# Rotary embedding on one core: whole 4 MB batches in five slots in place of 2 MB half batches in nine

## Chip, cores, metric

The kernel runs on one core of one Trainium2 chip. The metric is the device time of one execution in microseconds; most runs of one kernel agree within 0.3%.

## The reference, cut to what matters

```python
# x: (8, 2048, 8, 64) float32; cos, sin: (2048, 32) float32
x1, x2 = x[..., :32], x[..., 32:]
out1 = x1 * cos - x2 * sin        # cos, sin broadcast over batch and head
out2 = x1 * sin + x2 * cos
return np.concatenate([out1, out2], axis=-1)
```

33.55 MB come in, 33.55 MB go out, and the tables are 0.52 MB. Two multiplies and one add per element are all the work.

## The kernel before

Sequence positions lie on the partitions, 16 of them in each, so that one batch is 128 rows of 32 KB. A slab is half of that: 16 KB rows, 2 MB. It is loaded into one of nine slots, computed in place, and stored.

```python
SL = 8; n_half = R // SL; SLAB = SL * HD; UNIT = 4 * HD; NBUF = 9     # HD = 512 columns
slabs = [(b, l) for l in range(n_half) for b in range(B)]             # 16 slabs

def load(i):                       # all loads on the sync queue
    ...
    for lo, n in spans(cuts(i)):   # slab 0 in 256, 256, 512 KB and 1 MB, others whole
        nc.sync.dma_start(out=xt[:, lo : lo + n], in_=xv[b, :, l * SLAB + lo : ...])
        if i == 0 and lo == 0:
            nc.sync.dma_start(out=sin_sb, in_=sin_src)

nc.scalar.dma_start(out=cos_sb, in_=cos_src)
for i in range(NBUF):
    load(i)
```

A tile is 2048 columns (UNIT). There are three kinds. In A, GpSimd makes t2 = x swapped times sin (two instructions), VectorE makes t1 = x times cos and adds them. In B the add is done by TensorE (two products with the identity into PSUM) and ScalarE copies it back. In C VectorE makes both products and TensorE adds; GpSimd has nothing to do.

```python
kinds = {}
for i in (5, 10):
    kinds |= {(i, 0): "C", (i, UNIT): "B"}

def rotate(i, lo, n):
    ...
    if kind != "C":
        for u, tab in ((1, sin_sb), (0, nsin)):
            nc.gpsimd.tensor_mul(out=t2u[...], in0=xu[..., 1 - u, :], in1=rep(tab, H))
    keep(nc.vector.tensor_mul(out=t1, in0=xk, in1=rep(cos_ps, 2 * H)))
    if kind == "A":
        keep(nc.vector.tensor_add(out=xt, in0=t1, in1=t2))
    ...

for i in range(last + 1):          # stores on the ACT queue, two slabs late
    ...
    for lo, n in spans(pieces(i)):
        rotate(i, lo, n)
        if i == last:
            store(i, lo, n)
    if LAG <= i < last:
        store(i - LAG, 0, SLAB)
    if i > LAG and i - LAG - 1 + NBUF <= last:
        load(i - LAG - 1 + NBUF)
```

## Time and profile before

| | before |
|---|---|
| time, median | 164.75 us (164.62 to 164.78) |
| span of the profiled execution | 163.0 us |
| VectorE / GpSimd busy | 143.4 / 139.4 us |
| VectorE's last add ends | 155.0 us |
| transfers between 60 and 150 us | 431 GB/s |

### The profile page before, as it was taken

How to read it: one execution, taken by the hardware profiler on the slowest of the kernel's cores; microseconds unless marked ns; L12 is line 12 of the kernel's file. 1: busy time of each engine (PE TensorE's matmuls, PEld its weight loads, DVE VectorE, ACT ScalarE, POOL GpSimd, SP SyncE). 2: the span in 40 equal slices, each digit the busy share in tenths (PEclk: the TensorE clock that was granted, in tenths of full speed). 3: DMA queues.
4: the chain of work that ended last, by engine and by line, in shares of the span. 5: the costliest groups of instructions: out<-in, count | busy, mean ns of one | idle time of the engine just before them, and what ended most of it. 6: DMA issues, size and time to landing. Idle time of an engine off the chain costs nothing. (4 is left out here: it accounts for less than half of the span.)

```text
span 163.0 us, 480 instructions
## 1 busy us (share of the span) xinstructions
PE 33.3 (20%) x64; PEld 13.4 (8%) x64; DVE 143.4 (88%) x71; ACT 12.0 (7%) x20; POOL 139.4 (86%) x74
## 2 busy tenths in 40 slices
PE   0000000000000079993000000899920000000000
PEld 0000000000000024440000000244400000000000
DVE  0587999999999999999899999999999999999900
ACT  3300000000000002232000000022410000000000
POOL 1599999999999999799999999956999999995000
PEclk9999999999999999999555555579997555555555
DMA  4999999999999999999999999999999999999995
GB/s 137 383 432 442 406 398 426 438 438 418 438 434 426 430 434 430 426 434 438 422 428 438 424 422 446 430 414 446 434 422 430 442 422 422 446 426 430 434 402 207
DMA packets 5763, 67.66 MB, mean 415 GB/s; under 512 B 640, under 2 KB 640, under 8 KB 1664
## 3 DMA queue, kind: packets, MB, share of 16 engines
q1 hardware_dynamic: 2880, 33.82, 49.5%
q10 hardware_dynamic: 2880, 33.82, 48.7%
q14 instruction: 3, 0.02, 0.0%
HBM read 34.08 MB, written 33.55 MB: 415 GB/s over the span
## 5 line engine op out<-in xcount | busy, mean ns | idle before, releaser
L138 POOL TENSOR_TENSOR t<-xt,sin_sb 128x1024 f32<-128x1024 f32 (+2 forms) x34 | 70.7, 2081 | 10.8 <-DVE xt L151 6.3
L144 DVE TENSOR_TENSOR t<-xt,cos_ps 128x2048 f32<-128x2048 f32 (+2 forms) x36 | 73.9, 2056 | 1.0
L138 POOL TENSOR_TENSOR t<-xt,nsin 128x1024 f32<-128x1024 f32 (+2 forms) x34 | 70.8, 2082 | 0.0
L151 DVE TENSOR_TENSOR xt<-t,t 128x2048 f32<-128x2048 f32 (+2 forms) x32 | 64.8, 2025 | 5.6 <-POOL t L138 2.1
L172 PE MATMUL o<-t,eye 128*128 128x512 f32 x16 | 11.3, 800 | 85.8 <-DVE t L144 85.8
L176 ACT COPY xt<-o 128x512 f32<-128x512 f32 x8 | 4.7, 586 | 94.5 <-DVE t L144 55.3
L172 PEld LDWEIGHTS o<-t,eye 128*128 128x128 f32 x16 | 3.9, 256 | 90.6 <-issue 90.6
L156 PE MATMUL o<-t,eye 128*128 128x512 f32 x16 | 8.2, 592 | 0.0
L157 PE MATMUL o<-t,eye 128*128 128x512 f32 x16 | 8.2, 592 | 0.0
L173 PE MATMUL o<-t,neye 128*128 128x512 f32 x8 | 6.2, 862 | 0.2 <-DVE t L161 0.2
L158 ACT COPY xt<-o 128x512 f32<-128x512 f32 x8 | 4.7, 586 | 9.0 <-PE o L157 9.0
L108 DVE COPY cos_ps<-cos_sb 128x512 f32<-128x512 f32 x1 | 0.7, 694 | 5.0 <-DMA cos_sb<-in_cos_dram 5.0
L161 DVE TENSOR_TENSOR t<-xt,sin_ps 128x2048 f32<-128x2048 f32 x2 | 4.6, 2281 | 0.0
L173 PE MATMUL o<-t,eye 128*128 128x512 f32 x8 | 4.1, 592 | 0.0
L157 PEld LDWEIGHTS o<-t,eye 128*128 128x128 f32 x16 | 3.0, 190 | 3.8 <-issue 3.8
L156 PEld LDWEIGHTS o<-t,eye 128*128 128x128 f32 x16 | 3.0, 190 | 3.8 <-issue 3.8
L173 PEld LDWEIGHTS o<-t,neye 128*128 128x128 f32 x8 | 2.0, 278 | 4.9 <-issue 3.3
L173 PEld LDWEIGHTS o<-t,eye 128*128 128x128 f32 x8 | 1.5, 190 | 1.9 <-issue 1.9
L106 ACT ACT_TABLE_LOAD x1 | 1.3, 1283 | 1.2 <-PEq L215 1.2
L106 ACT ACTIVATE nsin<-sin_sb 128x512 f32<-128x512 f32 x1 | 0.6, 630 | 3.2 <-DMA sin_sb<-in_sin_dram 3.2
L109 ACT COPY sin_ps<-sin_sb 128x512 f32<-128x512 f32 x1 | 0.6, 579 | 0.0
L96 POOL MEMSET eye<- 128x128 f32 x1 | 0.2, 205 | 0.3 <-POOLq L215 0.3
(6 smaller groups left out, 1.0 us busy)
## 6 DMA issues: line engine op xcount, KB each, us to landing
xt<-in_x_dram SPq DMA_DIRECT2D x15, 2048.0 KB, 27.6
out_dram<-xt ACTq DMA_DIRECT2D x15, 2048.0 KB, 15.3
xt<-in_x_dram SPq DMA_DIRECT2D x1, 1024.0 KB, 7.8
out_dram<-xt ACTq DMA_DIRECT2D x1, 1024.0 KB, 10.3
xt<-in_x_dram SPq DMA_DIRECT2D x2, 256.0 KB, 4.3
xt<-in_x_dram SPq DMA_DIRECT2D x1, 512.0 KB, 5.8
out_dram<-xt ACTq DMA_DIRECT2D x1, 512.0 KB, 8.9
out_dram<-xt ACTq DMA_DIRECT2D x2, 256.0 KB, 7.6
```

The costliest lines, as they stand in the source:

```text
L106: nc.scalar.mul(nsin, sin_sb, -1.0)
L108: nc.vector.tensor_copy(cos_ps, cos_sb)
L138: nc.gpsimd.tensor_mul(out=t2u[:, :, u, :].rearrange("p (r h) d -> p r h d", h=H), in0=xu[:, :, 1 - u, :].rearrange("p (r h) d -> p r h d" ...
L144: nc.vector.tensor_mul(out=t1.rearrange("p (r k d) -> p r k d", r=nr, d=Dh), in0=xk, in1=rep(cos_ps[:, r0 : r0 + nr, :], 2 * H),)
L151: keep(nc.vector.tensor_add(out=xt, in0=t1, in1=t2))
L156: nc.tensor.matmul(o, eye, t1[:, cs], start=True, stop=False)
L157: nc.tensor.matmul(o, eye, t2[:, cs], start=False, stop=True)
L158: keep(nc.scalar.copy(xt[:, cs], o))
L161: nc.vector.tensor_mul(out=t2.rearrange("p (r k d) -> p r k d", r=nr, d=Dh), in0=xk, in1=rep(sin_ps[:, r0 : r0 + nr, :], 2 * H),)
L172: nc.tensor.matmul(o, eye, t1u[:, gs, u, :], start=True, stop=False)
L173: nc.tensor.matmul(o, eye if u else neye, t2u[:, gs, 1 - u, :], start=False, stop=True)
L176: keep(nc.scalar.copy(xu[:, gs, u, :], o.rearrange("p (g d) -> p g d", d=Dh)))
```

## The change

Its intent: fewer and longer transfers, the first MB of x ahead of the tables, stores as soon as a batch is done, and one TensorE tile in each of batches 1 to 5 rather than two in each of two slabs.

```diff
-    SL = 8 ... SLAB = SL * HD
+    ROW = R * HD
     UNIT = 4 * HD
-    NBUF = 9
+    NBUF = 5
-    t1s_pool = ... bufs=3
+    t1s_pool = ... bufs=2
-    def load(i): ...
-    nc.scalar.dma_start(out=cos_sb, in_=cos_src)
+    def load(b):
+        xt = xpool.tile([P, ROW], f32, tag="xt", name=f"xt{b}")
+        for lo, n in spans([UNIT, UNIT, 2 * UNIT] if b == 0 else [ROW]):
+            keep(nc.sync.dma_start(out=xt[:, lo : lo + n], in_=xv[b, :, lo : lo + n]))
+            if b == 0 and lo == 0:
+                keep(nc.sync.dma_start(out=cos_sb, in_=cos_src))
+                keep(nc.sync.dma_start(out=sin_sb, in_=sin_src))
-    for i in (5, 10):
-        kinds |= {(i, 0): "C", (i, UNIT): "B"}
+    for b, kind in ((1, "C"), (2, "B"), (3, "C"), (4, "B"), (5, "B")):
+        kinds[(b, 0)] = kind
     ...
+    def pieces(b):
+        if b == 0:
+            return [2 * HD, 2 * HD, UNIT, UNIT, UNIT]
+        if b == last:
+            return [UNIT, UNIT, UNIT, 2 * HD, 2 * HD]
+        return [UNIT] * 4
-    LAG = 2 ...
+    for b in range(B):
+        done = 0
+        outs = list(spans([2 * UNIT, UNIT, UNIT] if b == last else [ROW]))
+        for lo, n in spans(pieces(b)):
+            rotate(b, lo, n)
+            done = lo + n
+            while outs and sum(outs[0]) <= done:
+                store(b, *outs.pop(0))
+        if b + NBUF <= last:
+            load(b + NBUF)
```

More of the change, by code (lines that the diff above doesn't have):

```diff
@@ L28 @@
     R = S // P
-    SL = 8
-    n_half = R // SL
-    SLAB = SL * HD
+    ROW = R * HD
     UNIT = 4 * HD
-    NBUF = 9
+    NBUF = 5
     C = 512
+    last = B - 1
     xv = x.rearrange("b (q r) h d -> b q (r h d)", q=P)
@@ L45 @@
     o_pool = ctx.enter_context(tc.tile_pool(name="op", bufs=2, space=PSUM))
-    t1s_pool = ctx.enter_context(tc.tile_pool(name="t1s", bufs=3))
+    t1s_pool = ctx.enter_context(tc.tile_pool(name="t1s", bufs=2))
     xpool = ctx.enter_context(tc.tile_pool(name="xpool", bufs=NBUF))
@@ L56 @@
     sin_ps = tab_pool.tile([P, R, Dh], f32, tag="sp")
-    slabs = [(b, l) for l in range(n_half) for b in range(B)]
-    last = len(slabs) - 1
     xts = {}
-    def cuts(i):
-        if i == 0:
-            return [HD, HD, 2 * HD, UNIT]
-        return [SLAB]
-    def pieces(i):
-        if i == 0:
-            return [HD, HD, 2 * HD, UNIT]
-        if i == last:
-            return [UNIT, 2 * HD, HD, HD]
-        return [UNIT, UNIT]
     def spans(sizes):
@@ L78, in spans, with store @@
             lo += n
-    def load(i):
-        b, l = slabs[i]
-        xt = xpool.tile([P, SLAB], f32, tag="xt", name=f"xt{i}")
-        for lo, n in spans(cuts(i)):
-            nc.sync.dma_start(
-                out=xt[:, lo : lo + n],
-                in_=xv[b, :, l * SLAB + lo : l * SLAB + lo + n],
-            )
-            if i == 0 and lo == 0:
-                nc.sync.dma_start(out=sin_sb, in_=sin_src)
-        xts[i] = xt
-    nc.scalar.dma_start(out=cos_sb, in_=cos_src)
-    for i in range(NBUF):
-        load(i)
+    def load(b):
[5 more added lines that the diff above has]
+                keep(nc.sync.dma_start(out=sin_sb, in_=sin_src))
+        xts[b] = xt
+    def store(b, lo, n):
+        keep(nc.scalar.dma_start(out=ov[b, :, lo : lo + n], in_=xts[b][:, lo : lo + n]))
+    for b in range(NBUF):
+        load(b)
     nc.gpsimd.memset(eye, 0.0)
@@ L105 @@
     )
-    nc.scalar.mul(nsin, sin_sb, -1.0)
-    nc.scalar.mul(neye, eye, -1.0)
-    nc.vector.tensor_copy(cos_ps, cos_sb)
-    nc.scalar.copy(sin_ps, sin_sb)
+    keep(nc.scalar.mul(nsin, sin_sb, -1.0))
+    keep(nc.scalar.copy(sin_ps, sin_sb))
+    keep(nc.scalar.mul(neye, eye, -1.0))
+    keep(nc.vector.tensor_copy(cos_ps, cos_sb))
     def rep(a, n):
@@ L114, with rotate @@
     kinds = {}
-    for i in (5, 10):
-        kinds |= {(i, 0): "C", (i, UNIT): "B"}
-    def rotate(i, lo, n):
-        b, l = slabs[i]
-        kind = kinds.get((i, lo), "A")
-        xt = xts[i][:, lo : lo + n]
-        r0 = l * SL + lo // HD
+    for b, kind in ((1, "C"), (2, "B"), (3, "C"), (4, "B"), (5, "B")):
+        kinds[(b, 0)] = kind
+    def rotate(b, lo, n):
+        kind = kinds.get((b, lo), "A")
+        xt = xts[b][:, lo : lo + n]
+        r0 = lo // HD
         nr = n // HD
@@ L137, in rotate @@
             for u, tab in ((1, sin_sb), (0, nsin)):
-                nc.gpsimd.tensor_mul(
-                    out=t2u[:, :, u, :].rearrange("p (r h) d -> p r h d", h=H),
-                    in0=xu[:, :, 1 - u, :].rearrange("p (r h) d -> p r h d", h=H),
-                    in1=rep(tab[:, r0 : r0 + nr, :], H),
+                keep(
+                    nc.gpsimd.tensor_mul(
+                        out=t2u[:, :, u, :].rearrange("p (r h) d -> p r h d", h=H),
+                        in0=xu[:, :, 1 - u, :].rearrange("p (r h) d -> p r h d", h=H),
+                        in1=rep(tab[:, r0 : r0 + nr, :], H),
+                    )
                 )
@@ L175, in rotate @@
                     )
-                    keep(nc.scalar.copy(xu[:, gs, u, :], o.rearrange("p (g d) -> p g d", d=Dh)))
-    LAG = 2
-    def store(i, lo, n):
-        b, l = slabs[i]
-        keep(
-            nc.scalar.dma_start(
-                out=ov[b, :, l * SLAB + lo : l * SLAB + lo + n],
-                in_=xts[i][:, lo : lo + n],
-            )
-        )
-    for i in range(last + 1):
-        if i == last:
-            for k in range(i - LAG, i):
-                store(k, 0, SLAB)
-        for lo, n in spans(pieces(i)):
-            rotate(i, lo, n)
-            if i == last:
-                store(i, lo, n)
-        if LAG <= i < last:
-            store(i - LAG, 0, SLAB)
-        if i > LAG and i - LAG - 1 + NBUF <= last:
-            load(i - LAG - 1 + NBUF)
+                    keep(
+                        nc.scalar.copy(
+                            xu[:, gs, u, :], o.rearrange("p (g d) -> p g d", d=Dh)
+                        )
+                    )
+    def pieces(b):
[14 more added lines that the diff above has]
+            load(b + NBUF)
 _INS = ['x', 'cos', 'sin']
```

## The prediction

> **What bounds the kernel now.** I read the page's slices first, then the busy time in chosen windows, then the groups by form, the DMA view in short windows, and the chain of waits. The slices:
>
> ```profile
> span 163.0 us, 480 instructions
> ...
> PE 33.3 (20%) x64; PEld 13.4 (8%) x64; DVE 143.4 (88%) x71; ACT 12.0 (7%) x20; POOL 139.4 (86%) x74
> ...
> DMA  4999999999999999999999999999999999999995
> GB/s 137 383 432 442 406 398 426 438 438 418 438 434 426 430 434 430 426 434 438 422 428 438 424 422 446 430 414 446 434 422 430 442 422 422 446 426 430 434 402 207
> DMA packets 5763, 67.66 MB, mean 415 GB/s; under 512 B 640, under 2 KB 640, under 8 KB 1664
> ```
>
> Two engines are near 87%, but the DMA row has a 9 in every slice except the two at the ends. So bytes bound it, unless the last compute ends too late to hide. The windows show the same:
>
> ```profile
> 1.60:4.00 2.40, 0.00 (x0) 0.00 (x0) 0.00 (x0) 0.85 (x1) 0.00 (x0) 1.00 0.73 221
> 4.00:8.00 4.00, 0.00 (x0) 0.00 (x0) 2.18 (x4) 1.35 (x3) 2.26 (x4) 1.00 1.05 377
> ...
> 19.00:22.00 3.00, 0.00 (x0) 0.00 (x0) 2.90 (x2) 0.00 (x0) 3.00 (x2) 1.00 1.04 371
> 22.00:60.00 38.00, 2.04 (x2) 0.50 (x2) 37.03 (x18) 0.00 (x0) 38.00 (x18) 1.00 1.01 431
> 60.00:74.00 14.00, 13.85 (x30) 6.26 (x30) 13.62 (x8) 4.10 (x7) 12.82 (x7) 1.00 1.01 431
> ...
> 149.00:159.00 10.00, 0.00 (x0) 0.00 (x0) 5.57 (x7) 0.00 (x0) 1.39 (x2) 0.50 0.99 419
> 159.00:162.00 3.00, 0.00 (x0) 0.00 (x0) 0.00 (x0) 0.00 (x0) 0.00 (x0) 0.50 0.70 276
> ```
>
> The last column is GB/s. The plateau is 431 whatever mix of loads and stores runs. The necessary traffic is 33.55 MB in, 33.55 MB out and 0.52 MB of tables: 67.63 MB / 431 GB/s = 156.9 us. Time lost against the plateau, each as length x (1 - rate/431): 1.17 us (1.6 to 4), 0.50 (4 to 8), 0.42 (19 to 22), 0.17 (a 428 stretch, 86 to 110), 0.28 (149 to 159), 1.08 (the drain); sum 3.6. Then 1.6 + 156.9 + 3.6 = 162.1, and about 1 us of last receipt and finish makes the span of 163.0. A change that leaves the bytes alone can win back only some of those 3.6 us and a better plateau. The time is 164.75 against a span of 163.0: I add 1.75 us.
>
> The compute side, by form and from the chain of waits:
>
> ```profile
> L144 DVE TENSOR_TENSOR t<-xt,cos_ps 128x2048 f32<-128x2048 f32 x30 | 68.6, 2293 | 0.8
> L138 POOL TENSOR_TENSOR t<-xt,nsin 128x1024 f32<-128x1024 f32 x28 | 65.4, 2337 | 0.0
> ```
>
> ```profile
> 125.67 21.34 DMA out_dram<-xt
> ...
> 154.29 0.69 DVE xt L151
> ```
>
> VectorE's last add ends at 155.0, 8.0 us ahead of the end of the span. The stores are therefore a backlog in the queue, not waiting for VectorE. In the timeline starts are 2.36 us apart on VectorE (4.72 us for an ordinary tile of 2048 columns: multiply and add) and 2.28 on GpSimd (4.56 us for its two halves).
>
> **What the Trainium skill says.** "DMA: Bandwidth & Descriptors", section "Where 436 GB/s comes from", gives 435 GB/s as the fabric's ceiling; the plateau of 431 agrees, and leaves 1% above it at most. Its "Rules for kernel authors" ask for at least 1 MiB per DMA; before has 2 MB, so doubling should not matter much. "Why small descriptors are slow" names a fixed cost per packet. I find it in the packet records, where one row is one packet: median 84 ns for 2 KB, 159 for 4 KB, 309 for 8 KB, 611 for 16 KB, so doubling a row saves about 8 ns. "Issuing engines are not separate DMA queues" says that SP's and ACT's transfers interleave on the same 16 engines; the plateau is indeed the same with one queue active (60 to 74) and with both. So moving the tables to the sync queue costs no bandwidth.
>
> **The change part by part.**
>
> Rows. A 32 KB row should take 2 x 611 - 8 = 1214 ns, an estimate: 16 x 32768 B / 1214 ns = 432 GB/s against 429 from the same formula for 16 KB. That is 0.6%, at most 1.0 us of the 157; I take 0.5, as some rows stay small.
>
> Start. Before loads 256 KB pieces and tables, all in 2 KB rows (84 ns for what 8 KB rows do in 77); after has 8 KB rows for x first. I estimate 0.3 us less ramp. But the tables now come behind 1 MB: sin lands once 1.57 MB have moved. Before had moved 0.53 MB by 4 us, so at 377 GB/s that is 4 + 1.04/0.377 = 6.8 us, against 5.6 before. GpSimd starts at 7.0 instead of 5.74 and is what the first batch waits for: 4 operations at 1.22, then 6 at 2.28, end 25.5; VectorE's last add of batch 0 ends near 28.2. The first store goes out there instead of at 17.85. Loads alone run at the full plateau meanwhile, so nothing is lost yet.
>
> Work. Before has 28 ordinary tile-equivalents, 2 of the full TensorE kind (VectorE multiplies twice, no GpSimd) and 2 of the half kind (one multiply, TensorE adds). After has 27, 2 and 3. GpSimd stays at 30 x 4.56 = 137 us; VectorE drops from 30 x 4.72 + 2 x 2.36 = 146.3 to 29 x 4.72 + 3 x 2.36 = 144.0 with gaps. That is 2.3 us less, off the bound. TensorE and ScalarE have wide slack.
>
> Slots. Five slots of 4 MB replace nine of 2 MB. With both queues active each gets about 216 GB/s, 19.4 us for 4.19 MB. By hand, with an effective load start of 3.4 us: batches 0 and 1 (8.9 MB) at 24, batch 2 at 36 (first store packets near 31.5, since at full load 2 to 4 us pass from issue to first packet), then batches 3 to 7 at 55.5, 75, 94.4, 113.8 and 133.2. Stores 0 to 4 end at 51, 70, 90, 109 and 128.5. Load 5 needs store 0 (51, while load 4 still runs to 75), load 6 needs store 1 (70 against 94), load 7 store 2 (90 against 114). No load finds its slot late.
>
> Compute in that grid. VectorE ends batch 1 at 47, 2 at 63.5, 3 at 82.4, 4 at 99, 5 at 116, 6 at 136; GpSimd must wait for batches 4, 5, 6 and 7 to land (76, 95.4, 114.8, 134.2). Stores 0 to 6 are all issued before the preceding store has drained.
>
> Tail. Batch 7 lands at 134.2. GpSimd's tiles end at 138.8, 143.3, 147.9 and, in halves, 150.3 and 152.8; VectorE's adds end at 145.8 (first 2 MB store), 150.5 (1 MB) and 155.6 (1 MB). The stores left in the queue are: rest of batch 5 to 140.5, batch 6 to 150.3, then 155.1, 157.6 and 160.1 if no gap opens. The last is issued 2.0 us ahead of its turn, and needs 2 to 3 to get going: a gap of up to 1 us, where before had 256 KB pieces deep in a backlog. So VectorE's end is now close to deciding.
>
> Sum, by the same account as before: 1.6 + 156.4 (the better rows) + 1.3 (start) + 0.3 (a dip where the first store joins, and drifts) + 1.5 (tail and drain) = 161.1, plus 1.0 of receipt = 162.1. The wait for the last store may not overlap: 162.1 to 163. I take 162.1 + 1.75 = 163.8.
>
> **The rivals.**
> 1. DMA-bound throughout with a cleaner plateau: 32 KB rows give 433 to 434, no dip. Span 161, time 162.7. For: the law of packets and the ceiling of 435. Against: the dip and the drain have other causes.
> 2. The tail becomes compute-bound. A late batch-7 load, or 2 us of buffer waits on GpSimd (three temporary buffers; a TensorE tile holds one some 6 us longer), moves VectorE's end to 158; a 1 MB store then costs about 0.4 + 2 (start) + 2.4 + 1.1, so span 164, time 165.7. For: by my grid the last store is issued only 2 us ahead of its turn, where before the last of the backlog was issued 5 us ahead. Against: VectorE has some 3 us of idle time between batches that can absorb a delay.
> 3. Whole-batch granularity starves DMA in mid-kernel: all loads blocked by slots while stores wait for compute. That would cost about 4.7 us a tile, time 169 or more. For: five coarse slots instead of nine. Against: the grid has 20 us of slack at each reuse.
> 4. The change wins over 2% (161.4 or less). It would need a span of 159.7; even the skill's ceiling of 435 over all bytes, with no loss at the start, gives 1.6 + 155.5 + 1.5 + 1.0 = 159.6. Very unlikely.
>
> **Range and chances.** Rivals 1 and 2 bound the range from 162.6 to 165.6; the centre is 163.8, 0.6% faster. Faster by over 2%: 4%. Within 2%: 90%. Slower: 6%, nearly all from rival 3 or a stall that the grid does not know.
>
> **What would show it.** Plateau windows at 431 to 434 GB/s with one or both queues; a mean packet of about 1214 ns; no slice below 9 between the first and last two; GpSimd starting near 7 us and the first store near 28; VectorE ending near 155 to 156, with 6 to 7 us to the end of the span instead of 8. I am wrong if 32 KB rows are cut into smaller packets or run at another rate, if the two queues don't share equally (then batch 7 lands earlier or later than 134), if a slice in the middle falls to 5 or less, or if VectorE ends after 158.

## More of the kernel before

The one core has no other core beside it.

The prediction shows the page's rows and windows and reads them. One more view is needed to follow the result: the DMA view of the window 60 to 150 us. For each queue it gives packets, MB, and the time of its packets as a share of 16 engines.

```profile
DMA packets 2656, 38.78 MB, mean 431 GB/s; under 512 B 288, under 2 KB 288, under 8 KB 288
...
q10 hardware_dynamic: 1545, 22.69, 58.9%
q1 hardware_dynamic: 1109, 16.07, 41.8%
```

The packets under 512 B have 4 bytes and take 9 ns; the page has 640 of them for 40 transfers, 16 each, so I take them for the transfers' completion marks. The shares add up to 100.7% of 16 x 90 us, which is 1450 us; less 2.6 us for the small ones, over 2366 rows, a 16 KB row takes 612 ns. The median of the packet records is 611. Busy shares can come out a little above 100% because packets that straddle the window's edges are counted whole.

## The result, and the profile after

The changed kernel takes 164.18 us (164.0 to 164.46, 6 runs) against 164.68 (164.61 to 164.78, 6 runs) for the one before. The ratio is 0.997, 95% interval 0.9958 to 0.9983. The change is 0.3% faster.

The page of the changed kernel:

```profile
span 162.0 us, 463 instructions
...
PE 46.6 (29%) x80; PEld 18.6 (11%) x80; DVE 140.1 (86%) x66; ACT 14.3 (9%) x24; POOL 138.9 (86%) x70
...
DMA  5999999989899999999999999999999999999994
...
DMA packets 3170, 67.65 MB, mean 418 GB/s; under 512 B 352, under 2 KB 352, under 8 KB 608
```

DMA still fills every slice but the two at the ends. Two slices have an 8: the one from 32 to 36 us is met again below, and in the other (40 to 45 us) the account below finds nothing lost. The busy time of VectorE fell by 3.3 us, which shows nowhere in the span. The DMA view of 60 to 150 us, to set beside the one above:

```profile
DMA packets 1340, 38.90 MB, mean 432 GB/s; under 512 B 149, under 2 KB 149, under 8 KB 149
...
q10 hardware_dynamic: 794, 23.15, 59.6%
q1 hardware_dynamic: 544, 15.73, 40.5%
```

By the same working, 100.1% of 1440 us over some 1189 rows: a 32 KB row takes 1211 ns. The median of the packet records is 1213, where the prediction had 1214. Now windows of the start and of the middle (columns: window, length, busy time of each engine, granted clock, DMA share, GB/s):

```profile
1.60:4.00 2.40, 0.00 (x0) 0.00 (x0) 0.00 (x0) 0.41 (x1) 0.00 (x0) 1.00 0.95 294
4.00:8.00 4.00, 0.00 (x0) 0.00 (x0) 1.71 (x2) 1.09 (x3) 0.97 (x1) 1.00 1.02 416
27.00:36.00 9.00, 5.24 (x7) 2.01 (x8) 8.90 (x5) 0.58 (x1) 9.00 (x5) 1.00 0.97 371
60.00:150.00 90.00, 28.34 (x48) 11.42 (x48) 84.67 (x38) 7.02 (x12) 83.48 (x39) 0.67 1.00 432
```

The start is better than before (294 and 416 against 221 and 377). Between 27 and 36 us, where the first store joins the loads, there is a dip. A window counts a packet's bytes where it starts, which is coarse for 32 KB rows. For the account that follows I therefore spread each packet record's bytes evenly over its duration. Every gap is measured against the plateau between 60 and 125 us:

| us | before | after | e1 (16 KB rows) |
|---|---|---|---|
| first packet | 1.73 | 1.74 | 1.74 |
| 67.63 MB at the plateau | 157.15 (430.4 GB/s) | 156.34 (432.6) | 157.07 (430.6) |
| lost at the start, to 9 us | 1.72 | 0.97 | 0.93 |
| lost where the first store joins | 0.48 | 0.95 | 1.11 |
| lost in the rest, tail included | 0.79 | 0.71 | 0.57 |
| last packet ends | 161.85 | 160.69 | 161.40 |

The sums close within 0.02 us. The gain of 1.16 us in the last packet is 0.81 (rows) + 0.75 (start) - 0.47 (dip) + 0.08, to rounding. The chain of waits of the changed kernel ends so (start, length, what):

```profile
91.57 42.01 DMA xt<-in_x_dram
...
133.71 4.62 POOL t L121 x2
...
138.35 2.30 DVE xt L135
...
154.05 1.23 DVE xt L135
```

The last load is issued at 91.57 and lands at 133.6; GpSimd waits for it, VectorE for GpSimd; VectorE ends at 155.3, and 6.7 us of stores follow.

### The profile page after: what moved, and what is told of

Its sections match the earlier page's. It is cut to its first block, busy times and chain, and to the rows that moved or that the text cites. A ratio compares the mean times of both kernels' runs of the same rounds, so it can differ in the third digit from the quotient of the medians.

```text
span 162.0 us, 463 instructions
## 1 busy us (share of the span) xinstructions
PE 46.6 (29%) x80; PEld 18.6 (11%) x80; DVE 140.1 (86%) x66; ACT 14.3 (9%) x24; POOL 138.9 (86%) x70
## 3 DMA queue, kind: packets, MB, share of 16 engines
q10 hardware_dynamic: 1440, 33.56, 48.1%
## 4 chain that ended last, share of the span: by engine, by line
DMA 47%; DVE 37%; POOL 9%; issue 2%; SPq 1%; DVEq 0%; POOLq 0%; ACTq 0%
DMA xt<-in_x_dram 26%; DVE t L128 18%; DMA out_dram<-xt 18%; DVE xt L135 17%; POOL t L121 9%; DMA sin_sb<-in_sin_dram 3%; DVE t L145 1%; SPq L69 0%; SPq L67 0%; DVEq L135 0%; POOLq L121 0%; ACTq L74 0%
## 5 line engine op out<-in xcount | busy, mean ns | idle before, releaser
L121 POOL TENSOR_TENSOR t<-xt,sin_sb 128x1024 f32<-128x1024 f32 (+1 forms) x32 | 70.5, 2203 | 12.8 <-DMA xt<-in_x_dram 6.4
L128 DVE TENSOR_TENSOR t<-xt,cos_ps 128x2048 f32<-128x2048 f32 (+1 forms) x34 | 73.4, 2167 | 0.8
L121 POOL TENSOR_TENSOR t<-xt,nsin 128x1024 f32<-128x1024 f32 (+1 forms) x32 | 70.6, 2207 | 0.0
L135 DVE TENSOR_TENSOR xt<-t,t 128x2048 f32<-128x2048 f32 (+1 forms) x29 | 62.2, 2145 | 8.1 <-POOL t L121 5.6
L140 PE MATMUL o<-t,eye 128*128 128x512 f32 x24 | 16.3, 766 | 24.0 <-DVE t L128 24.0
L156 PE MATMUL o<-t,eye 128*128 128x512 f32 x16 | 11.3, 812 | 38.1 <-DVE t L128 38.1
L141 PE MATMUL o<-t,eye 128*128 128x512 f32 x24 | 15.3, 725 | 0.0
L142 ACT COPY xt<-o 128x512 f32<-128x512 f32 x12 | 7.0, 585 | 44.8 <-PE o L141 44.8
L140 PEld LDWEIGHTS o<-t,eye 128*128 128x128 f32 x24 | 5.6, 249 | 32.5 <-issue 32.5
L156 PEld LDWEIGHTS o<-t,eye 128*128 128x128 f32 x16 | 3.8, 257 | 43.0 <-POOL t L121 30.6
L161 ACT COPY xt<-o 128x512 f32<-128x512 f32 x8 | 4.7, 586 | 44.7 <-DVE t L128 26.6
L141 PEld LDWEIGHTS o<-t,eye 128*128 128x128 f32 x24 | 5.7, 239 | 8.0 <-issue 8.0
L157 PE MATMUL o<-t,neye 128*128 128x512 f32 x8 | 5.3, 766 | 0.2 <-DVE t L145 0.2
L157 PE MATMUL o<-t,eye 128*128 128x512 f32 x8 | 4.1, 592 | 0.0
L157 PEld LDWEIGHTS o<-t,eye 128*128 128x128 f32 x8 | 1.5, 190 | 1.9 <-issue 1.9
```

The lines of the kernel that those rows point to most:

```text
L121: nc.gpsimd.tensor_mul(out=t2u[:, :, u, :].rearrange("p (r h) d -> p r h d", h=H), in0=xu[:, :, 1 - u, :].rearrange("p (r h) d -> p r h d" ...
L128: nc.vector.tensor_mul(out=t1.rearrange("p (r k d) -> p r k d", r=nr, d=Dh), in0=xk, in1=rep(cos_ps[:, r0 : r0 + nr, :], 2 * H),)
L140: nc.tensor.matmul(o, eye, t1[:, cs], start=True, stop=False)
L141: nc.tensor.matmul(o, eye, t2[:, cs], start=False, stop=True)
L142: keep(nc.scalar.copy(xt[:, cs], o))
L156: nc.tensor.matmul(o, eye, t1u[:, gs, u, :], start=True, stop=False)
```

## The experiments

Twelve kernels ran (one of them, f1, is the changed kernel once more), all with right results. Unless the label says otherwise, "before" on the same chips took 164.6 to 164.8 us. The end of VectorE's last add, the last packet and the span are from the profiled execution of each.

**e1_rows16.** Each whole transfer is cut in two of 2 MB with 16 KB rows.

```diff
-[UNIT, UNIT, 2 * UNIT] if b == 0 else [ROW]
+[UNIT, UNIT, 2 * UNIT] if b == 0 else [ROW // 2] * 2
+# store(b, ...) likewise twice, each half
```

> The changed kernel with every whole-batch transfer cut into two of 2 MB with 16 KB rows, both issued at the place of the one. Theory A (the plateau is set by the cost of a row): a 16 KB row takes 611 ns, the plateau falls from 433-434 to 431 GB/s, 67.1 MB then take 0.9 us more, time 165.1 us (0.5 to 1.3 us over the changed kernel), which takes back more than the whole gain over the kernel before. Rival (the gain came from the start and from fewer transfers, rows don't matter): time within 0.3 us of 164.2.

Measured: 164.60 us, ratio 0.9993 (0.998 to 1.0007). The changed kernel itself did not run on this chip. The two kernels nearest to it that did, e2 and e3, have 0.9952 and 0.9953, so e1 stands some 0.7 us above them. By the ratios it stands only 0.2 us (f1) to 0.4 us above the changed kernel on other chips, but by the spans (162.7 to 162.9 against 161.9 to 162.3) 0.8 us. The 165.1 expected was too high. The DMA view of 60 to 150 us:

```profile
DMA packets 2672, 38.78 MB, mean 431 GB/s; under 512 B 304, under 2 KB 304, under 8 KB 304
...
q10 hardware_dynamic: 1468, 21.43, 55.6%
q1 hardware_dynamic: 1202, 17.33, 45.0%
```

Rows are back at 611 ns and the plateau at 430.6. In the table above it differs from the changed kernel by 0.73 us in the plateau's term and by 0.71 in the last packet. Theory A holds in kind: the rows give 0.7 us. The edit does two things more: it doubles the number of transfers, and the first half of a store now goes out as soon as its own tiles are done (the first at 18.92 us instead of 28.30, so the dip comes earlier too). Together these show no cost: start 0.04 and rest 0.14 less, the dip 0.16 more.

**e2_four_slots.** `NBUF = 5` becomes 4.

> Four slots of 4 MB in place of five. Theory A (by the grid of the prediction each slot comes back early enough): load 4 is issued when store 0 lands (52.8 us) and needs some 3 us to its first packet, 55.9, against 54.6 when load 3 ends; the stores fill the gap alone, so time 164.2, at most 0.3 more. Rival (coarse slots starve the loads): load 7 lands 1 to 4 us later and the time is 165.2 to 168. Also: if the dip of the DMA rate around 29 to 34 us comes from the depth of the load queue when the first store joins, it shrinks here from 0.9 us of lost transfer to under 0.5; if not it stays.

Measured: 163.90 us, ratio 0.9952 (0.994 to 0.9965), span 161.9. Load 4 was issued at 52.75 and had its first packet at 56.59, 1.8 us after load 3's last; the stores filled the gap and no rate fell. The fifth slot is worth nothing. The dip stays at 0.99 us, so the depth of the load queue does not make it.

**e6_three_slots.** `NBUF = 3`.

> Three slots. By the grid of the prediction load 3 then waits for store 0, which ends 16 us after load 2 has ended, both queues run dry around 44 to 47 us, and from then on each load starts when a store ends and its compute starts when it lands: VectorE ends near 168, time 172 to 178 us. Rival (the slots have room even so): under 167.

Measured: 178.47 us, ratio 1.0833 (1.0819 to 1.0848); 0.5 us above the range expected. VectorE ended at 171.8, where 168 was expected. Between 43 and 47 us the transfers fall to 131 GB/s, both queues being empty for a while, and the waits of GpSimd show who pays (columns: who waited for whom, us in total, times, longest):

```profile
POOL t L121 <- DMA xt<-in_x_dram: 23.2, 3, 11.2
```

This is the prediction's third rival, and it is real; but it begins between three and four slots, not at five.

**e3_no_b5.** The TensorE tile of batch 5 becomes an ordinary tile (`(5, "B")` is taken out).

> The TensorE tile of batch 5 is made an ordinary tile, which gives VectorE 2.36 us more. Theory A (VectorE's end is only just hidden): VectorE ends at 157.6 instead of 155.3, the last store is issued as the queue runs dry and needs some 2 us to start, span 1.5 to 2.5 us longer, time 165.7 to 166.7. Rival (the backlog of stores still covers it, or the idle time of VectorE takes it up): time within 0.4 us of 164.2.

Measured: 163.95 us, ratio 0.9953 (0.994 to 0.9965). My theory A failed here: VectorE ended at 155.7, not 157.6. In the changed kernel VectorE waits for GpSimd 5.6 us in all, partly in batch 5, and batch 7 cannot begin before its load lands at 133.6. The 2.4 us fell into idle time. So this run did not move the quantity it was to test.

**f4_late_vector.** Work is added where nothing can absorb it: the cos multiply of the last batch's first tile is done three times.

```diff
+        if b == last and lo == 0:
+            for _ in range(2):
+                keep(nc.vector.tensor_mul(out=t1, in0=xk, in1=rep(cos_ps, 2 * H)))
```

> The multiply of the first tile of the last batch is done three times, 4.6 us of VectorE work added where nothing can absorb it. VectorE ends near 159.9. Theory A (slack of VectorE's end is about 1 to 2 us before the store queue runs dry): the last store is issued at 160, flows at 160.9 and the span is 2.8 to 3.8 us longer, time 167 to 168. Rival (the slack is 4 us or more, VectorE far from the bound): less than 1 us longer.

Measured: 167.02 us, ratio 1.0134 (1.0119 to 1.0149), span 164.9. From the timeline:

```profile
138.32 4.63 DVE L137 TENSOR_TENSOR t<-xt,cos_ps 128x2048 f32<-128x2048 f32 x2
```

VectorE's last add ends at 160.1, the last store is issued there, its first packet flows 0.84 us later, its last ends 2.67 us after that, and the span 1.3 us later still: 4.8 us in all. Moving VectorE's end by 4.8 us cost 2.9 us of span. Theory A holds.

**f3_no_tensor.** No TensorE tile at all.

> No TensorE tile in any batch; all 32 tiles ordinary. GpSimd then has 32 x 4.56 = 146 us from 7.0 on and ends near 153 without ever waiting for a load, VectorE's last add near 155.8, as late as now. Theory A (bytes bound, compute hidden): time equal to the changed kernel within 0.3 us. Rival (the TensorE tiles carry part of the gain): VectorE ends 4 us or more later and the time is 2 us or more longer.

Measured: 167.96 us, ratio 1.0193 (1.0179 to 1.0207). The rival was right and my sum wrong: I had counted GpSimd (its end at 153.9 came as expected) and not VectorE, which does 32 x 4.72 = 151 us from 6.9 on and, with 3.4 us of waits and gaps, ends at 161.3.

The end of the chain of waits (start, length, what):

```profile
160.06 1.23 DVE xt L135
```

Without TensorE tiles the five-slot kernel is bound by VectorE. The three B tiles take 7 us off it, and e3 shows that two are enough. The next run shows that more is not better.

**e5_tail_early.** The first tiles of batches 6 and 7 become B tiles as well.

> The first tiles of batches 6 and 7 also go to TensorE. VectorE's last add ends 1 to 1.5 us earlier, near 154. Theory A (VectorE's end has 1.7 us of slack in the changed kernel, the stores decide): time equal within 0.3 us. Rival (the end of VectorE decides already): 1 us or more faster.

Measured: 165.92 us, ratio 1.0074 (1.0056 to 1.0092): neither theory. Four runs took 165.7 to 165.9 us with spans of 164.0 to 164.1, two took 166.5 to 166.7 with 164.8; the profile is of one of the two. In it VectorE ends at 159.7, 4.4 us later, though it has 4.7 us less to do. From the waits:

```profile
DVE xt L135 <- POOL t L121: 15.6, 7, 3.3
...
POOL t L121 <- DVE xt L135: 5.3, 3, 2.4
```

In the changed kernel these waits were 5.6 and 0.5. A B tile holds one of GpSimd's three result buffers until TensorE has read it. The two buffers left tie GpSimd to VectorE in turns: at 147.55 GpSimd had waited 2.40 us for an add, and VectorE then waited 2.42 us for that product. That the buffers are the cause is read from the waits; no run with more buffers was made.

These runs give one line for the end. VectorE's last add against the span:

| | VectorE ends | span | difference |
|---|---|---|---|
| f1 (changed kernel again) | 155.2 | 161.8 | 6.6 |
| after | 155.3 | 162.0 | 6.7 |
| e3_no_b5 | 155.7 | 162.2 | 6.5 |
| e2_four_slots | 156.1 | 161.9 | 5.8 |
| e4_old_start | 157.7 | 162.4 | 4.7 |
| e5_tail_early | 159.7 | 164.8 | 5.1 |
| f4_late_vector | 160.1 | 164.9 | 4.8 |
| f3_no_tensor | 161.3 | 166.1 | 4.8 |

Up to 156 the span does not follow VectorE; from 157.7 on it is VectorE's end plus 4.7 to 5.1. The two meet near 161.9 - 4.8 = 157.1: the changed kernel has about 1.8 us of slack. Left out are e1, g1 and e6, whose transfers changed, and f2 and h1, which lie with the first four (155.3 and 156.4, span 161.9 both).

**e4_old_start.** The start of the kernel before: small first pieces of x, loaded and computed, sin after the first, cos on the ACT queue.

```diff
-[UNIT, UNIT, 2 * UNIT] if b == 0
+[HD, HD, 2 * HD, UNIT, 2 * UNIT] if b == 0      # sin after the first, cos on ACT
```

> The start of the kernel before in the changed kernel: x in pieces of 256, 256, 512 KB, 1 MB, 2 MB, sin after the first piece, cos on the ACT queue. Theory A (only bytes lost at the ramp count): VectorE and GpSimd start near 5.7 us instead of 7.0, batch 0 ends about 1 us earlier, but small rows cost 0.2 to 0.5 us of transfer: time 164.4 to 164.7. Rival (the late tables cost time in the changed kernel): 163.2 to 163.8. If the dip near 29 to 34 us came from the first use of the ACT queue for a transfer, it is gone here.

Measured: 164.33 us, ratio 0.9975 (0.9962 to 0.9988); about 0.4 us above e2 and e3 on the same chip. The account has 1.52 us lost at the start against 0.97: the old start costs 0.55 us of transfer, and I put that down to its small 2 KB rows. But the dip is 0.43, as small as before, and that alone would make up for it. The rest makes the difference, 1.23 us against 0.71. The earlier tables let the first store go out 1 us earlier (27.34). Load 7 then lands at 136.0 instead of 133.6, GpSimd waits 10.0 us for loads instead of 6.4, and VectorE ends at 157.7, which is past its slack. That the earlier stores hold back the load is the likely link, not a tested one.

**f1_again and f2_cos_on_act.** The changed kernel once more, and with only cos on the ACT queue.

> The changed kernel as it is, to stand on the same chip as the next three: time 163.9 to 164.3 us, ratio 0.995 to 0.998. The dip of the DMA rate where the first store joins (0.9 us of transfer lost between 29 and 35 us in its first profile) should be there again; if it is random it will be elsewhere or of another size.

> Only cos goes back to the ACT queue. In four profiles in which the first store is the first transfer of the ACT queue the dip costs 0.9 to 1.1 us, in two in which cos went that way it costs 0.5. Theory B (the first use of a queue costs the difference): dip 0.5, time 0.3 to 0.5 us below the changed kernel on the same chip. Rival (the dip depends on something else that differed, such as the row size or when the store comes): dip 0.9 or more, time equal within 0.2.

Measured: f1 164.31 us (164.0 to 164.69), ratio 0.998 (0.9965 to 0.9995); f2 164.01 us, ratio 0.9952 (0.994 to 0.9965). The dip is 1.05 us in f1, so it is not random, and 0.87 in f2, near the rival's "0.9 or more" and far from 0.5 (h1, with the same edit, has 0.79). Theory B falls: the first use of the queue does not make the dip, though 0.1 to 0.2 us of it may go with it. The spans (161.8 and 161.9) are alike, and the intervals of the ratios touch at 0.9965; f2's 0.3 us is not established.

**g1_early_store.** Batch 0 is stored in four 1 MB pieces as its tiles finish (`[UNIT] * 4 if b == 0`).

> Batch 0 is stored in four pieces of 1 MB with 8 KB rows, each as soon as its tiles are done, the first near 13 us instead of all at 28. Theory C (the dip when the first store joins costs about a row or two of each engine, so it shrinks with the row of the joining store): dip 0.5 us or less, time 0.2 to 0.6 us below the changed kernel (163.6 to 164.0). Rival (the dip depends on the loads that are in flight): 0.9 again, at the new place, time equal.

Measured: 164.60 us (163.8 to 164.9), ratio 0.9977 (0.9956 to 0.9998). Two of the six runs took 163.8 to 163.9 us with a span of 161.8, as theory C said; four took 164.5 to 164.9, and the profile is of one of these. In it the dip fell to 0.12 as theory C said, but the time did not follow, so neither account is complete. The DMA view of 17.3 to 27.4 us, while the first small store runs beside a load:

```profile
q1 hardware_dynamic: 127, 3.64, 83.9%
q10 hardware_dynamic: 121, 0.99, 23.1%
```

Both queues sent about as many packets, but the load's are 32 KB and the store's 8 KB. The store queue got 21% of the bytes, near the 1 in 5 that one row each in turn gives. The first MB took 10.2 us, batch 0 was out at 62.6 instead of 51.2, and load 5 was issued at 63.1 instead of 52.8. From 60 to 125 us the rate was 430.4, which is 0.81 us more for all bytes, and in the rest 1.37 us were lost instead of 0.71. The last packet ended at 161.29, 0.60 later: the gain of the dip was more than given back. Why two runs escaped this is open, as neither was profiled.

**h1_both.** Four slots and cos on the ACT queue.

> Four slots and cos on the ACT queue together, each of which measured 0.3 us below the changed kernel (ratios 0.9952 against 0.997 and 0.998), with intervals that overlap. If both differences are real and add, the time is 163.4 to 163.7 us, ratio 0.992 to 0.994. If they are within the spread of runs and chips (theory A: nothing of the bound has moved, the span should stay at 161.8 to 162.0), the time is 163.8 to 164.3, ratio 0.995 to 0.998. VectorE's end near 156.2 keeps it just ahead of the point of 156.95 at which it would decide.

Measured: 163.66 us (163.53 to 164.31, 6 runs), ratio 0.9942 (0.9922 to 0.9963), span 161.9. The median lies in the range for "real and add", the ratio just outside it, the span where theory A has it, and the interval overlaps both; inconclusive. It is the lowest median and beats the kernel before, and it was not shown to beat the changed kernel: different chips, overlapping intervals, the same span.

## Why the prediction was right, point by point

- **Bound.** Right: transfers fill the span, and VectorE's 3.3 us less busy time (2.3 were predicted) bought nothing.
- **Rows.** Right in kind and short in size: 1214 ns was 1213, the 0.5 us taken was 0.8 (measured 0.81, and 0.73 when e1 undoes it). The full difference, which the prediction gave as at most 1.0, was the better guess.
- **Start.** The 0.3 us less ramp was 0.75. e4 shows that the start is the cause: that of before brings 0.55 of it back. GpSimd started at 7.03 as predicted, in part by luck: the bytes ran faster (416 GB/s between 4 and 8 us, not 377), but sin landed 0.36 us after its last packet (6.53), which the sum left out.
- **Slots and compute grid.** Right nearly everywhere: load 7 landed at 133.6 (134.2), the first store was issued at 28.3 (28.2), VectorE ended at 155.3 (155.6). The statement that slots return in time holds with one slot to spare (e2), and rival 3 is true of three slots (e6).
- **Tail.** Right. The sum's 1.5 us for tail and drain comes from windows, which give 1.36 for the kernel before; the packets give 0.79 before and 0.71 after, so the two must not be compared. As changes, 0.14 more was predicted, and 0.08 less came. The gap of up to 1 us ahead of the last store did not open: its first packet at 157.37 preceded the end of the one ahead, 157.67. The last packet ended at 160.69 (160.1 if no gap). The 2 us of start-up assumed in rival 2 are 0.84 when the queue is dry (f4).
- **Dip.** The sum's 0.3 for "a dip where the first store joins, and drifts" was 0.95 for the dip alone. The prediction counted on a smaller dip than before's 0.42, and it doubled. It is the term that failed most, and it takes back 0.47 us, more than half of the gain of the start. The sign "no slice below 9" failed with it.
- **Sum.** A span of 162.1 was predicted, 162.0 measured, and this is in part luck, as the errors cancel. As changes against the kernel before, predicted and measured: rows -0.5 and -0.81, start -0.37 and -0.75, dip and drifts -0.29 and +0.47, tail +0.14 and -0.08. The time missed by 0.4 us (163.8 against 164.18) because time minus span was 1.75 before and about 2.2 after. Runs have 1.7 to 2.2 there; why is open.
- **Rival 2** (compute tail) was the right danger: 1.8 us of slack, and the buffer waits that it named go with some 2 us in e5. **Rival 1** had the plateau nearly right (433 to 434, measured 432.6) and no dip, which is wrong.

What the dip is stays open. Over the runs it cost 0.43 to 1.33 us where the first store joins long loads. In the changed kernel load packets take 1.3 to 2.2 us there instead of 1.21, from about 1 us after the store's issue to its first packet. The queue's depth (e2), its first use (f2) and 16 KB rows (e1) do not remove it; e4 halves it and g1 nearly does away with it.

## What to carry to other kernels

Where transfers fill the span, write the time as first packet + bytes / plateau + losses; a change that leaves the bytes alone can only work on the plateau's last percent and on the losses, and two of them may cancel. Count each engine by itself when work is moved: here the TensorE tiles were needed (4 us without them), yet two more in the tail cost 2 us, through buffers as the waits suggest. Test a suspected slack by adding work at the very end, because work added earlier can vanish into idle time.

## What the Trainium skill lacked or had wrong

- "DMA: Bandwidth & Descriptors", "Where 436 GB/s comes from": it says the HBM side (some 358 GB/s) binds HBM to SBUF transfers, though it also calls a measured 425 GB/s near fabric rate. With one core running, both directions together held 430.4 to 432.6 GB/s here, near its fabric ceiling of 435: the 358 did not bind.
- The same page, "Why small descriptors are slow", names an overhead of some 3 cycles a packet and treats it as a matter of small ones. The records give 84, 159, 309, 611 and 1213 ns for rows of 2, 4, 8, 16 and 32 KB: 7 to 9 ns a row (twice one row's time less the time of the double row), still 0.7 us in 157 between 16 and 32 KB.
- The same page, "Queues, rings and completion order", has engines take turns by packet. It does not draw the consequence that bytes are shared by row size: 3.64 MB against 0.99 MB with 32 KB against 8 KB rows (g1).
- The same page, "Latency and other measured facts", gives 0.6 us to the first byte on these queues. From issue to first packet these runs show 1.0 us at the start, 0.84 with the queues dry (f4), and 4.0 for the first store beside loads (28.30 to 32.28 in the changed kernel).
- No page has the dip when a first store joins running loads: 0.43 to 1.33 us of transfer lost.
